# Moving the ConvFFN pool by 64 bytes, one adaLN unit from TensorE to VectorE, and widened products in the second half of a ConvFFN

## The chip, the cores and the metric

The kernel runs on one core of a Trainium2 chip. The metric is the device time of one execution in microseconds (us), lower is better; several executions are summed up by their median. Times inside the program come from one profiled execution and count from the start of its span.

## The reference

The program is one inference step of a two-layer diffusion backbone in float32 with D_MODEL 2048. Two groups of 128 tokens, a context pass and a denoising step, share all weights, so each weight block meets 256 token columns. Layer 0 mixes tokens with latent attention beside grouped-query attention, layer 1 with differential attention; each mixer is followed by a gated ConvFFN. Cut to what matters here:

```python
def conv_ffn(h, w_up, w_conv, b_conv, w_down):
    u = h @ w_up                                  # 2048 -> 2 x 5632
    up = jnp.pad(u, ((0, 0), (1, 1), (0, 0)))
    u = up[:, :-2] * w_conv[0] + up[:, 1:-1] * w_conv[1] + up[:, 2:] * w_conv[2] + b_conv
    gate, val = u[..., :D_FF], u[..., D_FF:]
    return (jax.nn.silu(gate) * val) @ w_down     # 5632 -> 2048

for l in range(DEPTH):                            # DEPTH = 2
    mod = jax.nn.silu(cond) @ w_ada[l] + b_ada[l] # 2048 -> 6 x 2048: the adaLN vectors
    sh1, sc1, gt1, sh2, sc2, gt2 = jnp.split(mod[:, None, :], 6, axis=-1)
    h = rmsnorm(x, g_norm_mix[l]) * (1 + sc1) + sh1
    x = x + gt1 * mixer(h)
    h = rmsnorm(x, g_norm_ffn[l]) * (1 + sc2) + sh2
    x = x + gt2 * conv_ffn(h, w_ffn_up[l], w_ffn_conv[l], b_ffn_conv[l], w_ffn_down[l])
```

## The kernel before

**Products.** Activations lie with features on partitions and 256 columns (128 of each group). To keep float32 accuracy with TensorE's fast format, each activation and each weight is split in a high part and a low part. A product of 2048 input features is 16 blocks of 128x128 weights with three matmuls each: `wh` with the high activations, `wh` with the low ones, `wl` with the high ones, so 48 matmuls of 256 columns, written by `gemm`. In every matmul the 128x128 weight block is loaded first, and 256 activation columns are streamed past it; the weight load of the next matmul runs beside the streaming of this one.

**Splitting the weights.** A weight tile `raw` of 1 MB arrives by a DMA from SP's queue. ScalarE casts it to `wh` (line 249) and VectorE subtracts to get `wl` (line 250), in halves of 1024 columns. In layer 0's ConvFFN a second way takes part of that off VectorE: of every five tiles, two have their second half split by transfer. `prepare` (lines 292 to 303) has ScalarE cast `farh` and write `-farh` into `farl`, and POOL issues a DMA that adds the raw weights from memory onto `farl`. These `farh`/`farl` buffers live in the ConvFFN's own pool.

**The ConvFFN** (`ffn`) goes through its 5632 hidden features in two halves (`q` = 0, 1). In each half `up` makes 22 gate and 22 value products (44 x 48 = 2112 matmuls of `hx` with up-weights), convolves them and splits the result into 22 tiles `g`; `down` makes 16 products of those 22 tiles with the down-weights (16 x 22 x 3 = 1056 matmuls). A list `wider` lets the first matmul of a few products stream 32, 16, 8, 4 and 2 columns more than 256. The added columns are not read. Before the change the list is used up in the first five of these products of each layer's first half. The mixer of layer 1 has a similar list, `push`, after each attention step.

**Addresses.** Each pool is laid out in the order in which its tags are first asked for; a pad of `SHIFT` = 320 bytes comes first in several pools. Within a partition the built program puts `hx` at byte 27264, the four `wh` from 104128 and the four `wl` from 120512 (steps of 4096), and in the ConvFFN pools of both layers `cv` from 148096 and the `g` tiles from 151168 (steps of 2048); in layer 0's also `farh` at 212608 and 216704 and `farl` at 220800 and 224896. Modulo 512 this is 128 for `hx`, `g`, `farh` and `farl`, and 192 for `wh` and `wl`. All steps from block to block and from high to low part are multiples of 512.

**The adaLN vectors** are made in units of 512 outputs of one (layer, vector j, quarter q), beside the other work, in two ways. A unit in `ROWS` is computed on TensorE: 16 matmuls of 512 columns (`sum_rows`), then a copy, four transposes and a reduction. A unit in `FEATS` is computed on VectorE alone, in eight steps of one fused multiply-and-sum over 128x2048 (line 499), for which four 1 MB tiles `araw` are loaded by SP. `pump` hands out these steps after each product at a fixed rate (`FRATE` for VectorE's, `RATE` for TensorE's), up to the limits in `FLIMIT` and `RLIMIT`. At three places (`modulated`) TensorE waits for a normalisation, and one `ROWS` unit is computed there between products.

**Order.** The framework's scheduler sets the order of each engine's instructions from its own simulation, except where `keep_order` pins it. A late `farl` therefore stops TensorE at the matmul that needs it.

Of the kernel before, what the change touches and what calls it, by code (L numbers as in the profile page):

```python
# [18 lines left out]
P = 128  # L19
# [32 lines left out]
NEARLY = _AT["bada"][0] + 2 * KD  # L52
WARM = 9
RATE = {"in0": 0.35, "in": 0.5, "in3": 0.25, "heads": 0.72, "out0": 0.62, "c": 0.36, "outc": 0.36}
FRATE = [{"up": 0.9, "down": 1.8}, {"up": 0.7, "down": 1.42}]
LEAD = (9, 3)
PEW = {"heads": 1.0, "out0": 1.0, "c": 1.0}
QUIET = [4, 3, 3]
LATE = 3
# [2 lines left out]
WIDER = (32, 16, 8, 4, 2)  # L62
# [15 lines left out]
ROWS = [(0, j, q) for q in range(4) for j in (1, 0)]  # L78
ROWS += [(0, j, q) for j in (2, 4) for q in range(4)]
ROWS += [(0, 5, 0)]  # L80
ROWS += [(1, 4, 0), (1, 3, 0)]
FEATS = [(0, 5, 1), (0, 5, 2), (0, 5, 3)]
FEATS += [(1, j, q) for j in (1, 0) for q in range(4)]
FEATS += [(1, 2, q) for q in range(4)]
FEATS += [(1, 5, q) for q in range(4)]
DEEP = [[(0, 3, q) for q in range(4)], [(1, 4, q) for q in range(1, 4)] + [(1, 3, q) for q in range(1, 4)]]
RLIMIT = {"ab": 16, "ffn0": 17, "c": 19, "ffn1": 19}
FLIMIT = {"ab": 0, "ffn0": 15, "c": 15, "ffn1": 19}

SIDE = {"in3": 0.4, "heads": 1.6, "out0": 1.8, "c": 2.2, "outc": 2.0}  # L90
UW = NT + 2
# [4 lines left out]
def step_kernel(ctx: ExitStack, tc: tile.TileContext, A: dict):  # L96
# [45 lines left out]
    def T_(pl, shape, tag, dt=F32, bufs=None):  # L142
        kw = {} if bufs is None else {"bufs": bufs}
        return pl.tile(shape, dt, tag=tag, name=nm(tag), **kw)
# [490 lines left out]
    def pump(rows, feats=0.0, until=None, beside=True):  # L635

        until = until or RLIMIT[stage[0]]
        step()
# [304 lines left out]
    def mixer_ab(hx, beside):  # L943
        l = 0
        with tc.tile_pool(name="ab", bufs=1) as ab:
# [297 lines left out]
            with tc.tile_pool(name="abh", bufs=1) as hp:  # L1243
                ada["pew"] = PEW["heads"]

# [91 lines left out]
    def out_ab(o, st, u, beside, rp):  # L1337
        l = 0
        rows = raw_rows(u, l, 1)
        ensure(l, 2)  # L1340
        ada["pew"] = PEW["out0"]
        W = Weights(A["w_out_ab"], KD, 1)
# [184 lines left out]
    def ffn(hx, W, ready, turn, l, st):  # L1527
        xh, xl = (lambda k: hx[:, k, :NT]), (lambda k: hx[:, k, NT:2 * NT])
        wider = list(WIDER)
        long = len(ready) > 3  # L1530

        def product():
            if ready:
                return ready.pop(0)
            if in_order:
                return gemm(W.chunk(), xh, xl, between=in_order.pop(0))
            if wider:
                n = NT + wider.pop(0)
                return gemm(W.chunk(), xh, xl, more=lambda k: hx[:, k, :n])
            return gemm(W.chunk(), xh, xl)  # L1540

        WD = Weights(A["w_down"][l], KQ, TB)
        cw = ada["cw"]
        with tc.tile_pool(name=f"ffn{l}", bufs=1) as fp, banks(f"pffn{l}") as pf:
            feat["home"], feat["pool"] = fp, pf
            feat["due"] = 0.0
            in_order = [{}, {}] + turn + [{}]
            T_(fp, [P, SHIFT // 4], "pad")

            def conv(m):  # L1550
                early = bool(ready)
                pin = keep_order if early else lambda i: i
                if len(ready) > 4 - 2 * long:
                    W.ahead(pin)
                ps = product()
                y = T_(fp, [P, NT], "cv", bufs=3)
                pin(act.activation(y, ps, AF.Identity, scale=cw[:, 1, m:m + 1], bias=cw[:, 3, m:m + 1]))  # L1557
                y3 = y.rearrange("p (g t) -> p g t", g=2)
                p3 = ps.rearrange("p (g t) -> p g t", g=2)
                pin(dve.scalar_tensor_tensor(out=y3[:, :, 1:], in0=p3[:, :, :T - 1],  # L1560
                                             scalar=cw[:, 0, m:m + 1], in1=y3[:, :, 1:],
                                             op0=ALU.mult, op1=ALU.add))
                pin(dve.scalar_tensor_tensor(out=y3[:, :, :T - 1], in0=p3[:, :, 1:],  # L1563
                                             scalar=cw[:, 2, m:m + 1], in1=y3[:, :, :T - 1],
                                             op0=ALU.mult, op1=ALU.add))
                if early and ready and not long:
                    W.ahead(pin)
                return y

            def up(q):  # L1570
                gs = []
                for i in range(q * KQ, (q + 1) * KQ):
                    rate = 0 if i < LATE else FRATE[l]["up"]
                    fine[0] = False
                    gate = conv(i)
                    pump(0, rate)
                    val = conv(NFF + i)
                    pump(0, rate)
                    act.activation(gate, gate, AF.Silu)
                    dve.tensor_tensor(out=val, in0=gate, in1=val, op=ALU.mult)  # L1580
                    g = T_(fp, [P, ROW], "g", F32R, bufs=KQ)
                    split(g[:, :NT], g[:, NT:2 * NT], val)
                    gs.append(g)
                    if i == LATE - 1:
                        load_row()
                return gs

            def down(gs, q):
                u, rows = None, None
                if q == NQ - 1 and l < NL - 1:  # L1590
                    u = raw_tile(keep, "hx")
                    rows = raw_rows(u, l + 1, 0)
                for c in range(KD):
                    quiet = q == NQ - 1 and c >= KD - QUIET[0]
                    fine[0] = quiet
                    if q == 0:
                        ensure(l, 5, [c // 4])
                    ps = gemm(WD.chunk(), lambda k: gs[k][:, :NT], lambda k: gs[k][:, NT:2 * NT])
                    if l == NL - 1 and q == NQ - 1 and c == KD - 1:
                        last_residual(ps, l, 1, c, st)  # L1600
                    else:
                        residual(ps, l, 1, c, st if q == NQ - 1 else None)
                    if rows:
                        rows(c)
                    if l == NL - 1 and q == NQ - 1 and c in EARLY:
                        act.activation(x[:, c], x[:, c], AF.Identity, scale=C("gfin")[:, c:c + 1])
                    pump(0, 0 if quiet else FRATE[l]["down"])
                return u

            for q in range(NQ):  # L1610
                if l == 0:
                    at, n = 2 * KQ * q, KQ * KD // TB
                    W.go_far(fp, at + LEAD[q], at + 2 * KQ, at + 2 * KQ)
                    WD.go_far(fp, n * q + 3, n * q + n, n * q + n - 6 * q)
                gs = up(q)
                u = down(gs, q)
            while feat["i"] < FLIMIT[stage[0]]:
                feature_step()
            return u
# [26 lines left out]
    with tc.tile_pool(name="cc", bufs=1) as cp, banks("pc") as ppool["ada"]:  # L1646
# [6 lines left out]
        st = stat_init()  # L1653
        ada["pew"] = PEW["c"]
        u = mixer_c(cp, hx, W, begun[0], st)
# [155 lines left out]
```

## Time and profile before

| | us |
|---|---|
| median of 3 executions | 2321.04 (2319.64 to 2321.44) |
| the profiled execution: time | 2326.57 |
| its span | 2324.8 |
| TensorE busy in the span | 2292.3 (99%) |
| VectorE, ScalarE, POOL busy | 1888.9, 1231.6, 227.8 |

In the profile an instruction's busy time overlaps the next one's on TensorE, since matmuls are pipelined; the pace of a stretch is read from the start times of successive matmuls, or from the length of a stretch and the number of matmuls that the code puts in it. Layer 0's ConvFFN runs from about 473 to 1193 us (its second half begins at 819), the mixer of layer 1 from about 1197 to 1595, and layer 1's ConvFFN from about 1615 to 2312 (first `down` from 1833.7, second `up` from 1953.4, second `down` from 2192.7). PE is the matmul stream, PEld the weight loads, SP and POOL issue DMAs.

### The profile page before, as it was taken

Reading aid. Unit: us, or ns where it says so; the run is one execution under the profiler, and the core shown is the slowest. Engines: PE = TensorE matmul, PEld = TensorE weight load, DVE = VectorE, ACT = ScalarE, POOL = GpSimd, SP = SyncE. Lnnn points to the kernel's source line nnn. Section 1 sums busy time; section 2 is a strip of 40 time slices with the busy share of each in tenths; the row PEclk is TensorE's granted clock in tenths of the full one; section 3 lists DMA queues with packets and bytes.
Section 4 is the critical chain, followed back from the end, with each engine's and each line's share of the span. In section 5 each row is a group of like instructions: output and inputs, shape, how many; then the busy total and the mean of one; then the engine's idle time right before and its main releaser. Section 6 shows DMA issues by size and latency. Waiting matters only on the chain.

```text
span 2324.8 us, 47335 instructions
## 1 busy us (share of the span) xinstructions
PE 2292.3 (99%) x19388; PEld 2209.0 (95%) x19388; DVE 1888.9 (81%) x2975; ACT 1231.6 (53%) x1999; POOL 227.8 (10%) x281
## 2 busy tenths in 40 slices
PE   8899999999999999999999999999999999999998
PEld 6788878999999999999999999999999999999998
DVE  4668979889888998989978989998999965666654
ACT  4346555675554455555565455557655434555543
POOL 0012111300000000000230000024000000000011
PEclk9999999999999999999999999999999999999999
DMA  9988879789889999998977887766767655555553
GB/s 380 366 335 307 327 287 366 290 296 305 293 301 318 350 318 305 304 311 291 325 262 268 338 277 272 257 217 214 253 259 269 257 200 198 188 195 200 188 194 127
DMA packets 106313, 639.68 MB, mean 275 GB/s; under 512 B 11440, under 2 KB 19568, under 8 KB 39536
## 3 DMA queue, kind: packets, MB, share of 16 engines
q1 hardware_dynamic: 99904, 614.11, 71.1%
q0 software_dynamic: 6192, 22.55, 5.3%
q8 instruction: 152, 2.49, 0.4%
q14 instruction: 65, 0.53, 0.1%
HBM read 631.86 MB, written 4.75 MB: 274 GB/s over the span
## 4 chain that ended last, share of the span: by engine, by line
PE 94%; DVE 2%; DMA 2%; POOL 1%; ACT 1%; issue 0%; SPq 0%; DVEq 0%; ACTq 0%; POOLq 0%
PE acc L111 89%; PE ada L111 3%; PE att L111 2%; DMA kvb<-w_ada 1%; DVE wl L250 1%; PE att L114 1%; DMA farl<-w_up 0%; PE misc L111 0%; DMA araw<-w_ada 0%; POOL dev L833 0%; DVE hx L551 0%; PE ada L114 0%; DVE x L1668 0%; POOL hxc L837 0%; ACT wh L249 0%
## 5 line engine op out<-in xcount | busy, mean ns | idle before, releaser
L111 PE MATMUL acc<-hx,wh 128*128 128x256 f32 (+1 forms) x6784 | 1188.8, 280 | 5.2 <-ACT wh L249 1.7
L249 ACT CAST wh<-raw 128x1024 fp32r<-128x1024 f32 (+2 forms) x791 | 749.7, 961 | 765.7 <-PE acc L111 637.4
L250 DVE TENSOR_TENSOR wl<-raw,wh 128x1024 fp32r<-128x1024 f32 (+2 forms) x791 | 876.3, 1121 | 264.6 <-ACT wh L249 260.8
L111 PEld LDWEIGHTS acc<-hx,wh 128*128 128x128 f32 x6784 | 1032.8, 189 | 24.0 <-issue 8.5
L111 PE MATMUL acc<-hx,wl 128*128 128x256 f32 (+1 forms) x3392 | 946.0, 279 | 4.7 <-DVE wl L250 4.4
L111 PEld LDWEIGHTS acc<-hx,wl 128*128 128x128 f32 x3392 | 639.5, 189 | 8.1 <-DVE wl L250 6.3
L111 PE MATMUL acc<-g,wh 128*128 128x256 f32 x2608 | 452.7, 279 | 0.0
L111 PEld LDWEIGHTS acc<-g,wh 128*128 128x128 f32 x2608 | 396.6, 189 | 0.0
L111 PE MATMUL acc<-g,wl 128*128 128x256 f32 x1304 | 362.5, 278 | 0.0
L499 DVE CUSTOM_DVE_ANT_0 junk<-araw,condb 128x2048 f32<-128x2048 f32 x152 | 349.5, 2299 | 1.3 <-DMA araw<-w_ada 1.3
L111 PEld LDWEIGHTS acc<-g,wl 128*128 128x128 f32 x1304 | 245.1, 188 | 0.0
L111 PE MATMUL acc<-hxc,wh 128*128 128x256 f32 (+1 forms) x1056 | 188.9, 281 | 0.0
L111 PEld LDWEIGHTS acc<-hxc,wh 128*128 128x128 f32 x1056 | 161.7, 188 | 1.0 <-issue 0.8
L212 POOL TENSOR_TENSOR sqacc<-sqacc,sq 128x256 f32<-128x256 f32 x62 | 73.1, 1178 | 878.6 <-ACT sq L208 878.4
L111 PE MATMUL acc<-hxc,wl 128*128 128x256 f32 (+1 forms) x528 | 146.8, 278 | 0.0
L1557 ACT ACTIVATE cv<-acc,convw 128x256 f32<-128x256 f32 x169 | 94.3, 558 | 19.9 <-PE acc L111 19.7
L111 PEld LDWEIGHTS acc<-hxc,wl 128*128 128x128 f32 x528 | 99.5, 189 | 0.2
L111 PE MATMUL acc<-wh,hxc 128*128 128x256 f32 (+1 forms) x512 | 94.3, 282 | 0.8 <-DVE nt L844 0.8
L111 PE MATMUL acc<-hx,farh 128*128 128x256 f32 x480 | 88.6, 285 | 0.0
L551 DVE CUSTOM_DVE_ANT_0 hx<-block,condb 128x1024 fp32r<-128x1024 f32 x65 | 79.4, 1222 | 6.8 <-DMA block<-w_ada 6.3
L1563 DVE SCALAR_TENSOR_TENSOR cv<-acc,convw,cv 128x254 f32<-128x254 f32 x169 | 81.1, 480 | 3.5
L1560 DVE SCALAR_TENSOR_TENSOR cv<-acc,convw,cv 128x254 f32<-128x254 f32 x169 | 80.5, 477 | 3.3 <-ACT cv L1557 3.3
(275 smaller groups left out, 2280.3 us busy)
## 6 DMA issues: line engine op xcount, KB each, us to landing
raw<-w_up SPq DMA_DIRECT2D x176, 1024.0 KB, 5.3
araw<-w_ada SPq DMA_DIRECT2D x136, 1024.0 KB, 6.9
raw<-w_down SPq DMA_DIRECT2D x88, 1024.0 KB, 5.0
raw<-w_in_c SPq DMA_DIRECT2D x48, 1024.0 KB, 6.6
block<-w_ada SPq DMA_DIRECT2D x41, 512.0 KB, 5.9
raw<-w_in_ab SPq DMA_DIRECT2D x18, 1024.0 KB, 9.2
raw<-w_out_ab SPq DMA_DIRECT2D x16, 1024.0 KB, 8.1
raw<-w_out_c SPq DMA_DIRECT2D x16, 1024.0 KB, 6.1
```

The source lines that it names most:

```text
L111: return self.placed(nc.tensor.matmul(*a, **kw))
L114: return self.placed(nc.tensor.transpose(*a, **kw))
L212: eng.tensor_tensor(out=st["acc"], in0=st["acc"], in1=sq, op=ALU.add)
L249: pin(act.copy(out_hi, src))
L250: pin(dve.tensor_tensor(out=out_lo, in0=src, in1=out_hi.bitcast(F32), op=ALU.subtract))
L499: keep_order(dve.tensor_tensor_reduce(out=T_(feat["pool"], [P, D], "junk"), in1=feat["row"][:, c], in0=feat["raw"].rearrange("p g n -> p ( ...
L551: keep_order(dve.tensor_tensor_reduce(out=self.junk, in0=self.raw, in1=self.row[:, c].rearrange("p (g n) -> p g n", g=2), scale=1.0, scala ...
L1557: pin(act.activation(y, ps, AF.Identity, scale=cw[:, 1, m:m + 1], bias=cw[:, 3, m:m + 1]))
L1560: pin(dve.scalar_tensor_tensor(out=y3[:, :, 1:], in0=p3[:, :, :T - 1], scalar=cw[:, 0, m:m + 1], in1=y3[:, :, 1:], op0=ALU.mult, op1=ALU.add))
L1563: pin(dve.scalar_tensor_tensor(out=y3[:, :, :T - 1], in0=p3[:, :, 1:], scalar=cw[:, 2, m:m + 1], in1=y3[:, :, :T - 1], op0=ALU.mult, op1=A ...
```

## The change

Three things change.

1. A pad of `FARAWAY` = 16 floats (64 bytes), tag `farpad`, is asked for right behind the first pad in the ConvFFN pool, in both layers. In the built program this moves every buffer of that pool by 64 bytes: `cv`, all `g` tiles and the broadcast condition in both layers, and `farh` (212672, 216768) and `farl` (220864, 224960) in layer 0. Modulo 512, `g`, `farh` and `farl` are now at 192; `hx` stays at 128, `wh` and `wl` at 192.
2. Unit (1,4,0) goes from `ROWS` to `FEATS`: eight more steps on VectorE in layer 0's ConvFFN, with rates 0.95 and 1.9 in place of 0.9 and 1.8 to fit them in. Unit (1,3,0) takes its place inside `modulated` ahead of layer 1's mixer, and no unit is left to TensorE within that mixer.
3. In layer 0, the second half's first five `up` products are widened too.

```diff
-FRATE = [{"up": 0.9, "down": 1.8}, {"up": 0.7, "down": 1.42}]
+FRATE = [{"up": 0.95, "down": 1.9}, {"up": 0.7, "down": 1.42}]
 LEAD = (9, 3)
+FARAWAY = 16
...
-ROWS += [(1, 4, 0), (1, 3, 0)]
+ROWS += [(1, 3, 0)]
...
-FEATS += [(1, 2, q) for q in range(4)]
+FEATS += [(1, 2, q) for q in range(4)] + [(1, 4, 0)]
...
-RLIMIT = {"ab": 16, "ffn0": 17, "c": 19, "ffn1": 19}
-FLIMIT = {"ab": 0, "ffn0": 15, "c": 15, "ffn1": 19}
+RLIMIT = {"ab": 16, "ffn0": 17, "c": 18, "ffn1": 18}
+FLIMIT = {"ab": 0, "ffn0": 16, "c": 16, "ffn1": 20}
...
             T_(fp, [P, SHIFT // 4], "pad")
 
+            T_(fp, [P, FARAWAY], "farpad")
...
+                if l == 0 and q:
+                    wider.extend(WIDER)
                 gs = up(q)
```

On TensorE the order changes at the border between layer 0's first `down` (products of `g`) and its second `up` (products of `hx`). A row is a source line, an operation, the tile written, the moving and the weight tile, and the shape. Before, the last `down` product ends and the `up` product begins:

```order
L111 MATMUL acc_9711<-g_8228,farh_9536 128x256 x2
L111 MATMUL acc_9711<-g_8228,farl_9537 128x256
L111 MATMUL acc_9711<-g_8357,farh_9536 128x256 x2
L111 MATMUL acc_9711<-g_8357,farl_9537 128x256
L111 MATMUL acc_9796<-hx_5342,wh_9788 128x256 x2
L111 MATMUL acc_9796<-hx_5342,wl_9789 128x256
```

At the same place of the changed kernel, eight blocks earlier:

```order
L112 MATMUL acc_9721<-g_7267,wl_9718 128x256
L112 MATMUL acc_9721<-g_7405,farh_9545 128x256 x2
L112 MATMUL acc_9810<-hx_5342,wh_9802 128x288
L112 MATMUL acc_9810<-hx_5342,wh_9802 128x256
L112 MATMUL acc_9810<-hx_5342,wl_9803 128x256
L112 MATMUL acc_9721<-g_7405,farl_9546 128x256
L112 MATMUL acc_9721<-g_7544,farh_9545 128x256 x2
```

The first three matmuls of the `up` product, the one with 288 columns among them, now stand inside the last `down` product, and 22 matmuls with `far` weights follow them. The next widened matmul (272 columns) opens the second `up` product.

On TensorE in layer 1's mixer, within a product between two attention steps, before (`ada` is the sum of a unit, `araw` its weights):

```order
L111 MATMUL acc_15414<-hxc_14510,wl_15407 128x256
L111 MATMUL acc_15414<-hxc_14510,wh_15410 128x256
L111 MATMUL ada_15441<-araw_14970,condw_79 32x512 x4
L111 MATMUL ada_15441<-araw_15040,condw_79 32x512 x4
L111 MATMUL acc_15414<-hxc_14510,wh_15410 128x256
L111 MATMUL acc_15414<-hxc_14510,wl_15411 128x256
```

And in the changed kernel:

```order
L112 MATMUL acc_15436<-hxc_14537,wl_15429 128x256
L112 MATMUL acc_15436<-hxc_14537,wh_15432 128x256 x2
L112 MATMUL acc_15436<-hxc_14537,wl_15433 128x256
L112 MATMUL acc_15436<-hxc_14537,wh_15432 128x256 x2
L112 MATMUL acc_15436<-hxc_14537,wl_15433 128x256
```

The unit's matmuls are gone here and at a second place further on, and with them its four transposes.

On VectorE at the end of layer 0's ConvFFN the last steps of the moved unit stand where there were none (`junk` is the step's scratch output, `hx` the next layer's operand being written, `x` the residual), in the changed kernel:

```order
L251 TENSOR_TENSOR wl_14087<-raw_13980,wh_14086 128x512 x2
L500 ISA junk_13796,mod_77<-araw_13794,condb_5751 128x2048
L500 ISA mod_77 128x1
L870 SCALAR_TENSOR_TENSOR x_76<-acc_13994,mod_77,x_76 128x128 x2
L251 TENSOR_TENSOR wl_14093<-raw_13980,wh_14092 128x512 x2
L251 TENSOR_TENSOR wl_14175<-raw_14070,wh_14174 128x512 x2
L500 ISA junk_13890,mod_77<-araw_13794,condb_5751 128x2048
```

Before, at the same product:

```order
L250 TENSOR_TENSOR wl_14060<-raw_13953,wh_14059 128x512 x2
L869 SCALAR_TENSOR_TENSOR x_76<-acc_13967,mod_77,x_76 128x128 x2
L250 TENSOR_TENSOR wl_14066<-raw_13953,wh_14065 128x512 x2
L728 SCALAR_TENSOR_TENSOR hx_12805<-x_76,scl_78,hx_12805 128x128 x2
L250 TENSOR_TENSOR wl_14148<-raw_14043,wh_14147 128x512 x2
```

The last two steps of the unit now stand behind the place where all such steps had ended before.

## The prediction

> **What bounds the kernel now.** I read the page first, then the chain of waits in order of time, then TensorE's start times where the chain's pace changes, then each ConvFFN phase in the table of stretches. The page:
>
> ```profile
> PE 2292.3 (99%) x19388; PEld 2209.0 (95%) x19388; DVE 1888.9 (81%) x2975; ACT 1231.6 (53%) x1999; POOL 227.8 (10%) x281
> L499 DVE CUSTOM_DVE_ANT_0 junk<-araw,condb 128x2048 f32<-128x2048 f32 x152 | 349.5, 2299 | 1.3 <-DMA araw<-w_ada 1.3
> ```
>
> TensorE is the bound almost everywhere, so what counts is its pace per matmul. The chain (start us, length us, what) shows three long pieces of product matmuls:
>
> ```profile
> 473.16 205.57 PE acc L111 x1749
> 678.73 11.17 DMA farl<-w_up
> 689.95 505.71 PE acc L111 x4265
> ...
> 1597.25 715.33 PE acc L111 x6296
> ```
>
> 505.71 us over 4265 matmuls is 118.6 ns each, in layer 0's ConvFFN; 715.33 over 6296 is 113.6 ns, in layer 1's. The shape is the same, yet 5 ns differ. TensorE's timeline (start us, length, instruction; x2 is two merged) shows where the faster pace is lost:
>
> ```profile
> 505.35 0.39 PE L111 MATMUL acc<-hx,wh 128*128 128x256 f32 x2
> ...
> 505.69 0.40 PE L111 MATMUL acc<-hx,farh 128*128 128x256 f32 x2
> 505.93 0.28 PE L111 MATMUL acc<-hx,farl 128*128 128x256 f32 x1
> 506.05 0.40 PE L111 MATMUL acc<-hx,farh 128*128 128x256 f32 x2
> 506.29 0.28 PE L111 MATMUL acc<-hx,farl 128*128 128x256 f32 x1
> ...
> 508.56 0.40 PE L111 MATMUL acc<-hx,wh 128*128 128x256 f32 x2
> ...
> 508.92 0.40 PE L111 MATMUL acc<-hx,wh 128*128 128x256 f32 x2
> ```
>
> Up to 505.69 three matmuls take 0.34 us (113 ns each). With the first `far` weights they take 0.36 (120 ns: 505.93 to 506.29), and when `wh` and `wl` return, the pace does not: it stays near 118. So there are two paces for the same operands, and a `far` block throws TensorE out of the faster one. A widened matmul brings it back, in layer 1's ConvFFN with 288 columns and in its mixer with 272:
>
> ```profile
> 1350.58 0.40 PE L111 MATMUL acc<-hxc,wh 128*128 128x256 f32 x2
> ...
> 1350.94 0.41 PE L111 MATMUL acc<-hxc,wh 128*128 128x272 f32 x2
> ...
> 1351.64 0.39 PE L111 MATMUL acc<-hxc,wh 128*128 128x256 f32 x2
> ...
> 1351.98 0.39 PE L111 MATMUL acc<-hxc,wh 128*128 128x256 f32 x2
> ...
> 1631.93 0.40 PE L111 MATMUL acc<-hx,wh 128*128 128x256 f32 x2
> ...
> 1632.28 0.41 PE L111 MATMUL acc<-hx,wh 128*128 128x288 f32 x2
> ...
> 1633.00 0.39 PE L111 MATMUL acc<-hx,wh 128*128 128x256 f32 x2
> ...
> 1633.34 0.28 PE L111 MATMUL acc<-hx,wh 128*128 128x256 f32 x1
> ```
>
> 0.35 to 0.36 us per three before, 0.34 after. The phases, from the table of stretches (from:to, length, PE busy and count, PEld, DVE, ACT, POOL, clock, DMA share, GB/s):
>
> ```profile
> 505.70:687.50 181.80, 181.80 (x1540) 181.77 (x1538) 159.17 (x206) 102.26 (x139) 10.37 (x12) 1.00 0.90 302
> 693.70:819.00 125.30, 125.30 (x1058) 125.30 (x1058) 112.66 (x133) 54.28 (x54) 6.90 (x8) 1.00 0.95 332
> 819.00:1068.60 249.60, 249.60 (x2115) 249.60 (x2114) 225.32 (x289) 139.03 (x189) 13.86 (x16) 1.00 0.90 306
> 1068.60:1193.20 124.60, 124.60 (x1058) 124.60 (x1057) 112.97 (x162) 67.02 (x113) 21.28 (x19) 1.00 0.84 293
> 1633.70:1833.70 200.00, 200.00 (x1767) 200.00 (x1766) 184.65 (x240) 109.23 (x149) 0.00 (x0) 1.00 0.70 256
> 1833.70:1953.40 119.70, 119.70 (x1059) 119.70 (x1058) 77.94 (x94) 47.38 (x47) 0.00 (x0) 1.00 0.60 213
> 1953.40:2192.70 239.30, 239.30 (x2114) 239.30 (x2113) 162.15 (x218) 126.83 (x174) 0.00 (x0) 1.00 0.56 194
> 2192.70:2312.40 119.70, 119.70 (x1058) 119.70 (x1057) 61.08 (x85) 52.49 (x73) 16.20 (x14) 1.00 0.47 163
> ```
>
> They are, in order: layer 0's first `up` from its first `far` block, its first `down`, second `up`, second `down`; then layer 1's first `up` from the widening on and its other three. Layer 1 keeps 113.3 ns (239.3/2112) through all four, with VectorE 92% busy in the first of these rows. Layer 0's second `up` has 118.2 (249.6/2112); with its 16 `far` halves (two tiles of five, from the fourth on) of 24 matmuls at 120, the other 1728 take 117.8.
>
> **What sets the pace.** Modulo 512 bytes, the streamed `hx` and `g` are at 128 and `wh`, `wl` at 192, 64 apart, while `far` is at 128, 0 apart. The address of the weights alone is not it: in the transposed products of layer 1's mixer the weights are `hxc` (128 modulo 512), the streamed tile is `wh`, 64 apart again, and the faster pace holds:
>
> ```profile
> 1338.05 0.39 PE L111 MATMUL acc<-wh,hxc 128*128 128x256 f32 x2
> ...
> 1338.39 0.39 PE L111 MATMUL acc<-wh,hxc 128*128 128x256 f32 x2
> ```
>
> I take it that 0 apart costs 120 ns and that 64 apart has both paces.
>
> **The change part by part.** The pad moves `far`, which mends layer 0's `up`: `hx` at 128 against `wh` and `far` at 192. But it moves `g` as well, in both layers: `g` at 192 against `wh`, `wl` and `far` at 192 is 0 apart in every matmul of every `down`.
>
> - Layer 0, first `up`: 1540 matmuls at 113.3 instead of 181.8 us: 174.5, so -7.3.
> - Layer 0, first `down`: 1056 at 120 is 126.7 against 125.3: +1.4. Second: 126.7 against 124.6: +2.1.
> - Layer 0, second `up`: the 288-column matmul stands within the last `down` product with 22 `far` matmuls behind it, so I count the first product at 118. The 272-column one that opens the second product flips the pace, as at 1350.94. 2112 at 113.3 plus 48 x 5 ns plus about 0.1 for the added columns is 239.7 against 249.6: -9.9.
> - Layer 1, first `down`: 126.7 against 119.7: +7.0. It leaves the slower pace, and nothing widens the second `up` of layer 1. So that one takes 2112 x 117.8 = 248.8 against 239.3: +9.5. Second `down`: +7.0.
> - The unit taken off TensorE, from the chain within the mixer:
>
> ```profile
> 1269.39 5.72 PE acc L111 x49
> 1275.12 1.85 PE ada L111 x16
> ...
> 1307.20 1.85 PE ada L111 x16
> ...
> 1310.57 11.16 PE acc L111 x97
> ...
> 1347.56 16.60 PE acc L111 x145
> ...
> 1384.20 5.84 PE acc L111 x50
> ```
>
> From 1269.39 to 1310.57 are 41.18 us and to 1347.56 another 36.99, where a head without the unit takes 36.64 (1347.56 to 1384.20): 4.5 + 0.4 = -4.9.
>
> - The unit put on VectorE: 8 x 2.30 = 18.4 us. In layer 0's second `up`, 44 x 0.05 = 2.2 of these steps add 5.1 us to 225.3 while the phase shrinks to 239.7: 96% busy, from 90%. The 92% of layer 1's first `up` cost TensorE nothing, so I price it at 0, with little cover left. Its 4 MB of loads on SP's queue and the faster pace lift the DMA share from 0.90 to about 0.95, what the first `down` has now.
>
> What is late next are the `farl` transfers. One was late already (timeline, and the tile's line):
>
> ```profile
> DMA to landing us min/median/max: 5.3/8.4/12.1
> 689.95 0.38 PE L111 MATMUL acc<-hx,farl 128*128 128x256 f32 x1 [2.19 <-DMA farl<-w_up]
> ```
>
> With products 4% shorter and queues fuller, such a wait gets longer or comes again: between 0 and 2 us in the likely case; I take 0.6, nearer to nothing, since the profile has a single such wait.
>
> Sum: -7.3 + 1.4 - 9.9 + 2.1 + 7.0 + 9.5 + 7.0 - 4.9 + 0.6 = +5.5. The profiled execution took 2326.57, so it would take 2332.1; against the median of 2321.04 that is 2326.5. About 0.2% (4.6 us) is what a measurement of this kernel tells from no change.
>
> [...]
>
> **The rivals.**
>
> 1. *Harmless `g`* (faster). If both tiles at 192 do not disturb each other as both at 128 do, layer 0 runs at 113.3 throughout: -7.3 - 9.9 - 5.6 - 4.9 (each `down` at 119.7), less 4.9 for the unit: -32.6, so 2288. For it: no row shows both at 192. Against it: the distance is the same 0.
> 2. *Late transfers undo the gain* (slower). A wait at an early `far` block of an `up` throws TensorE into the slower pace until the next widening. If it comes at the first of the second `up`, some 9 of the 9.9 us go and 2.2 for the wait itself: 2338. It decides when a landing there takes longer than about 9 us: the one in the chain took 11.17, and TensorE waited 2.19 of them. The median is 8.4.
> 3. *Addresses don't matter*, `far` is slow for being written by transfers. Then the unit's -4.9 is left and a faster pace for the second `up` until its first `far` block, about 1 us: 2315. Against it: `farh`, which ScalarE writes as it writes `wh`, is as slow.
> 4. *Distance 0 costs only the slower pace*, 118, in a `down`. Each `down` then takes 1056 x 117.8 = 124.4: layer 0 gives -17.2 - 0.9 - 0.2, layer 1 +4.7 + 9.5 + 4.7, the unit -4.9: -4.3, so 2317, the lower edge of no change. Against it: 120 in the `far` run shown.
>
> **How the numbers follow.** Forecast 0.55 (within it the edge of 0.2% lies 0.8 us below the centre: 0.35 slower, 0.20 same); rival 1 0.15 (faster), rival 2 0.15 (slower), rival 3 0.07 (faster 0.06, same 0.01), rival 4 0.08 (same 0.05, faster 0.03). Together faster 0.24, same 0.26, slower 0.50. The range, 2314 to 2340, takes in all but rival 1. The likeliest case alone spans 2320 to 2333: a pace read wrong by 1 ns over the 4224 matmuls of `down` is 4.2 us, and the wait for `farl` may go (2.2) or come again (2.2).
>
> **What would show it.** Right: in layer 0's `up` phases 113 ns also in `far` blocks, 120 in all four `down` phases, 118 in layer 1's second `up`, mixer heads all near 36.6 us. Wrong: layer 1 still at 113.3 throughout (rival 1), `far` blocks of `up` still at 120 (rival 3), waits for `farl` early in an `up` (rival 2), or waits for `wl`, if VectorE at 96% runs dry.

## The result, and the profile after

The changed kernel took 2336.91 us (median of 5 executions, 2330.22 to 2338.53) against 2321.44 us for the kernel before in the same rounds (5 executions, 2319.64 to 2324.32). The ratio is 1.0062, with a 95% interval from 1.0045 to 1.0078: slower, by more than the 0.2% that a measurement can tell. The forecast was 2326.5, range 2314 to 2340; the side and the range were right, the centre was 10.4 us too low.

The profiled execution is the fastest of the five: 2330.22 us, span 2328.5, 3.7 us over the profiled one of before. What follows reads that execution. First the page: TensorE's busy time fell by 4.0 us though the span grew by 3.7.

```profile
PE 2288.3 (98%) x19352; PEld 2205.5 (95%) x19352; DVE 1904.0 (82%) x2990; ACT 1227.2 (53%) x1998; POOL 233.9 (10%) x281
```

The table of stretches of the changed kernel (from:to, length, then busy time and count of PE, PEld, DVE, ACT, POOL, then clock, DMA share, GB/s). The rows are layer 0's first `up` from its first `far` block, first `down`, second `up`, second `down`; then layer 1's first `down` and second `up`:

```profile
504.20:686.70 182.50, 179.05 (x1563) 178.37 (x1562) 166.12 (x216) 101.57 (x140) 10.37 (x12) 1.00 0.93 311
686.70:814.50 127.80, 127.56 (x1061) 127.16 (x1060) 117.92 (x138) 55.76 (x57) 6.89 (x8) 1.00 0.97 337
814.50:1063.90 249.40, 245.20 (x2111) 244.02 (x2110) 226.72 (x292) 137.86 (x188) 13.86 (x16) 1.00 0.92 310
1063.90:1190.60 126.70, 126.70 (x1058) 126.70 (x1058) 122.13 (x172) 66.97 (x115) 26.47 (x19) 1.00 0.88 304
...
1823.30:1950.00 126.70, 126.70 (x1059) 126.70 (x1057) 78.25 (x94) 47.08 (x47) 0.00 (x0) 1.00 0.56 203
1950.00:2189.40 239.40, 239.40 (x2115) 239.40 (x2114) 162.09 (x218) 126.82 (x174) 0.00 (x0) 1.00 0.55 193
```

Phase by phase, the difference between the two profiled executions adds up to the 3.7 us:

| stretch | before | after | difference |
|---|---|---|---|
| up to layer 0's ConvFFN (ends at) | 472.9 | 471.4 | -1.5 |
| first `up`, all of it | 220.8 | 215.3 | -5.5 |
| first `down` | 125.3 | 127.8 | +2.5 |
| second `up` | 249.6 | 249.4 | -0.2 |
| second `down` | 124.6 | 126.7 | +2.1 |
| between the ConvFFNs | 422.1 | 414.3 | -7.8 |
| layer 1: first `up` | 218.4 | 218.4 | 0.0 |
| first `down` | 119.7 | 126.7 | +7.0 |
| second `up` | 239.3 | 239.4 | +0.1 |
| second `down` | 119.7 | 126.7 | +7.0 |

Nothing is changed ahead of layer 0's ConvFFN; the other runs reach it between 472.6 and 473.5 us, so the first row is a difference between executions.

The two `down` phases of layer 1 cost 14 us, as forecast: 126.7/1056 is 120.0 ns a matmul, with no wait in them and every other engine less than 62% busy. The `far` blocks of layer 0's `up` do keep the faster pace now. In TensorE's timeline, three matmuls take 0.34 us on both sides of the border at 504.22:

```profile
503.77 0.28 PE L112 MATMUL acc<-hx,wl 128*128 128x256 f32 x1
...
504.11 0.28 PE L112 MATMUL acc<-hx,wl 128*128 128x256 f32 x1
504.22 0.39 PE L112 MATMUL acc<-hx,farh 128*128 128x256 f32 x2
504.45 0.28 PE L112 MATMUL acc<-hx,farl 128*128 128x256 f32 x1
```

What I had wrong is at the other border, in layer 1 from the first `down` to the second `up`, where nothing is widened:

```profile
1949.52 0.28 PE L112 MATMUL acc<-g,wl 128*128 128x256 f32 x1
...
1949.88 0.28 PE L112 MATMUL acc<-g,wl 128*128 128x256 f32 x1
1950.00 0.40 PE L112 MATMUL acc<-hx,wh 128*128 128x256 f32 x2
1950.24 0.28 PE L112 MATMUL acc<-hx,wl 128*128 128x256 f32 x1
...
1950.58 0.28 PE L112 MATMUL acc<-hx,wl 128*128 128x256 f32 x1
```

With the last triple of `g` and the first of `hx` the spacing is 0.36 us (1949.52, 1949.88, 1950.24), from then on 0.34 (1950.58): one triple behind the border TensorE is in the faster pace by itself.

Layer 0's second `up` gained nothing, though it too should run faster. Its idle time is one part. TensorE's waits in layer 0's ConvFFN were one, of 2.2 us, before (the 2.19 at 689.95); now they are nine (what was waited for: us in all, times, longest):

```profile
PE acc L112 <- DMA farl<-w_up: 3.8, 4, 1.5
PE acc L112 <- DVE wl L251: 2.1, 3, 0.9
PE acc L112 <- DVE cv L1566: 1.7, 2, 1.1
```

The other part is its pace, from the table of stretches with pieces of the second `up` that hold no wait:

```profile
840.00:890.00 50.00, 50.00 (x427) 50.00 (x426) 46.85 (x62) 30.19 (x42) 3.46 (x4) 1.00 0.98 342
900.00:950.00 50.00, 50.00 (x444) 50.00 (x443) 44.41 (x60) 27.56 (x38) 2.59 (x3) 1.00 0.95 302
968.00:1018.00 50.00, 50.00 (x427) 50.00 (x426) 42.99 (x56) 26.95 (x38) 3.46 (x4) 1.00 0.91 298
```

427 matmuls in 50 us are the slower pace, 444 the faster one. The phase began at the faster pace (178 matmuls in the 20 us from 817.00). Between the pieces the pace changes where TensorE is held up. At the first `far` block of the phase the third matmul, the first one that needs `farl`, takes 0.39 us instead of 0.28 and sets back what follows by 0.1 us (0.34 us from 838.64 to 838.98, then 0.46 to 839.44), and TensorE goes on at the slower pace. The trace names no wait there, but POOL issued the transfer of that `farl` at 828.37, and it took 10.6 us to land, until just when TensorE came to it. The wait that ends at 896.11, in the fifth block, brings it back to the faster one; the wait that ends at 966.05 leaves it at the slower one again. Timeline, and the line of the `farl` tile for that one transfer:

```profile
838.64 0.28 PE L112 MATMUL acc<-hx,wl 128*128 128x256 f32 x1
...
838.98 0.39 PE L112 MATMUL acc<-hx,farl 128*128 128x256 f32 x1
...
839.44 0.28 PE L112 MATMUL acc<-hx,farl 128*128 128x256 f32 x1
...
896.11 0.39 PE L112 MATMUL acc<-hx,farl 128*128 128x256 f32 x1 [0.33 <-DMA farl<-w_up]
...
966.05 0.39 PE L112 MATMUL acc<-hx,wl 128*128 128x256 f32 x1 [0.79 <-DVE wl L251]
```

```profile
DMA to landing us min/median/max: 10.6/10.6/10.6
```

### The profile page after: what moved, and what is told of

It reads as the page before. It is cut to its first block, busy times and chain, and to the rows that moved or that the text cites. A ratio compares the mean times of both kernels' runs of the same rounds, so it can differ in the third digit from the quotient of the medians.

```text
span 2328.5 us, 47301 instructions
## 1 busy us (share of the span) xinstructions
PE 2288.3 (98%) x19352; PEld 2205.5 (95%) x19352; DVE 1904.0 (82%) x2990; ACT 1227.2 (53%) x1998; POOL 233.9 (10%) x281
## 4 chain that ended last, share of the span: by engine, by line
PE 90%; DMA 4%; DVE 3%; ACT 1%; issue 1%; POOL 1%; SPq 0%; DVEq 0%; ACTq 0%; POOLq 0%
PE acc L112 85%; PE ada L112 2%; PE att L112 2%; DMA farl<-w_up 1%; DVE wl L251 1%; DMA kvb<-w_ada 1%; DVE junk L500 1%; DMA raw<-w_in_ab 1%; PE att L115 1%; DMA farl<-w_down 0%; DMA araw<-w_ada 0%; DMA raw<-w_up 0%; PE misc L112 0%; DVE hx L552 0%; ACT wh L250 0%
## 5 line engine op out<-in xcount | busy, mean ns | idle before, releaser
L112 PE MATMUL acc<-hx,wh 128*128 128x256 f32 (+1 forms) x6784 | 1175.8, 279 | 7.0 <-ACT wh L250 1.7
L112 PEld LDWEIGHTS acc<-hx,wl 128*128 128x128 f32 x3392 | 638.4, 188 | 11.1 <-DVE wl L251 9.3
L112 PE MATMUL acc<-g,wh 128*128 128x256 f32 x2608 | 469.9, 284 | 0.1
L112 PEld LDWEIGHTS acc<-g,wh 128*128 128x128 f32 x2608 | 406.9, 192 | 0.3 <-ACT g L250 0.3
L112 PE MATMUL acc<-g,wl 128*128 128x256 f32 x1304 | 368.9, 284 | 0.0
L500 DVE CUSTOM_DVE_ANT_0 junk<-araw,condb 128x2048 f32<-128x2048 f32 x160 | 367.0, 2294 | 0.0
L112 PEld LDWEIGHTS acc<-g,wl 128*128 128x128 f32 x1304 | 250.4, 192 | 0.0
L213 POOL TENSOR_TENSOR sqacc<-sqacc,sq 128x256 f32<-128x256 f32 x62 | 78.4, 1264 | 882.3 <-ACT sq L209 882.0
L300 ACT CAST farh<-raw 128x1024 fp32r<-128x1024 f32 x43 | 45.2, 1051 | 77.2 <-DMA raw<-w_up 59.8
L1566 DVE SCALAR_TENSOR_TENSOR cv<-acc,convw,cv 128x254 f32<-128x254 f32 x169 | 80.9, 479 | 2.9
```

Source lines behind the costliest of these rows:

```text
L112: return self.placed(nc.tensor.matmul(*a, **kw))
L213: eng.tensor_tensor(out=st["acc"], in0=st["acc"], in1=sq, op=ALU.add)
L300: act.copy(wh, raw[:, 8 * P:n * P])
L500: keep_order(dve.tensor_tensor_reduce(out=T_(feat["pool"], [P, D], "junk"), in1=feat["row"][:, c], in0=feat["raw"].rearrange("p g n -> p ( ...
```

## The experiments

The first four separate the parts of the change. `prepare` is the function that asks for the buffers of the transfers.

**e1: only the transfers' buffers move, `g` stays.** The changed kernel with the pad asked for behind `g` and ahead of `farh`:

```diff
+    padded = []
...
+                    if "far" not in padded:
+                        padded.append("far")
+                        T_(self.far, [P, FARAWAY], "farpad", bufs=1)
...
-            T_(fp, [P, FARAWAY], "farpad")
```

> The changed kernel with the 64-byte pad placed between g and the far buffers, so that far moves and g stays where it was; unit move and widening are kept. Theory A (the distance of streamed tile and weights sets the pace: 0 apart 120 ns, 64 apart 113 or 118): all four down phases leave 120, layer 1's two go from 126.7 back to 119.7 us, together -14.0, layer 0's two from about 127 to 120 at best, -14 more: 2336.9 - 28 = 2309, or up to 2316 if the faster down makes more farl transfers late. Rival B (the changed kernel's loss is the extra unit and its loads, not g): stays within 5 us of 2337.

Measured: 2317.07 us, ratio to before 0.9974 (0.9964 to 0.9985). The rows of layer 0's ConvFFN and of layer 1's first `down`:

```profile
473.50:1191.50 718.00, 700.24 (x6074) 697.50 (x6073) 660.22 (x853) 386.53 (x528) 55.91 (x57) 0.99 0.92 312
...
1827.50:1947.20 119.70, 119.70 (x1058) 119.70 (x1057) 77.96 (x94) 47.39 (x47) 0.00 (x0) 1.00 0.59 213
```

Layer 1's `down` phases are back at 119.7 and 119.6: the 14 us come from where `g` lies (`cv` and the broadcast condition stay with it, but TensorE reads neither in a `down`). The time is 1 us above the range of theory A and far from B. In layer 0 the products became 11.1 us shorter than in the changed kernel (TensorE busy 700.2 against 711.3), but the ConvFFN only 1.2 (718.0 against 719.2): 17.8 us are idle now.

**e2: the pad alone.** The kernel before with the pad where the change has it, without the moved unit and the wider products:

```diff
+FARAWAY = 16
...
+            T_(fp, [P, FARAWAY], "farpad")
```

> The kernel before with the pad of the change alone (g and far both move), no unit moved, no widening mid-way. Both theories: layer 1's down phases +7.0 each, layer 1's second up stays at 113 ns. What differs is layer 0's up. Theory A1 (the faster pace alone makes farl late): several waits of 0.5 to 2 us in the second up as in the changed kernel, which then takes about 249 us: 2321.4 + 14 + 3.5 - 6 = 2333. Theory A2 (the moved unit's steps and loads make farl late): at most two waits, second up about 241 us: 2321.4 + 14 + 3.5 - 7 - 9 = 2323.

Measured: 2332.75 us, ratio 1.0040 (1.0028 to 1.0053). Rows of layer 0's ConvFFN and of the stretch between:

```profile
472.70:1189.50 716.80, 708.89 (x6074) 707.46 (x6073) 644.57 (x835) 385.78 (x528) 59.85 (x57) 1.00 0.90 307
1189.50:1608.70 419.20, 417.83 (x3529) 408.37 (x3529) 376.58 (x673) 242.19 (x488) 74.93 (x92) 1.00 0.75 265
```

The pad alone makes the kernel slower: each `down` of layer 1 takes 126.7 us. The time is that of A1, but not for its reason: layer 0's second `up` took 244.1 us here, without any widened matmul, and not 249 as in the changed kernel.

**e3: the unit alone.** The kernel before with the unit on VectorE, its rates and limits as in the diff of the change, and no pad.

> The kernel before with unit (1,4,0) moved to VectorE, its rates and limits, and nothing else. If the unit's matmuls are all that counts: -4.9, 2316.5, with heads of the mixer all near 36.6 us and layer 0's ConvFFN as long as before (720 us from 473 to 1193). If the extra steps and loads cost TensorE waits there: 2321 or more, with waits for farl or wl in layer 0's ConvFFN.

Measured: 2321.60 us, ratio 0.9993 (0.9983 to 1.0002): no change, as the second expectation has it. The rows of layer 0's ConvFFN and of the stretch between:

```profile
473.30:1195.30 722.00, 717.60 (x6074) 716.55 (x6073) 660.41 (x853) 386.77 (x528) 60.35 (x57) 1.00 0.92 310
1195.30:1609.60 414.30, 412.67 (x3494) 406.55 (x3493) 375.41 (x670) 241.63 (x487) 76.72 (x92) 1.00 0.74 258
```

The stretch between is 7.8 us shorter than before, as in the changed kernel. Only 4.9 of that belong to the unit: e2, without it, has 419.2 there. The other 2.9 are the output projection of layer 1's mixer, 642 matmuls that ran at 118.5 ns before (76.1 us) and at 114.1 in the changed kernel (73.3 us). By the lengths of the stretch they had the faster pace here and in e2 too, and the slower one in e1, where it takes 417.7. The unit's gain on TensorE is real, and layer 0's ConvFFN gives part of it back: 722.0 us against 720.3, with 4.4 us idle (722.0 less 717.6) instead of 2.2.

**e4: only the transfers' buffers move, nothing else.** The kernel before with e1's pad.

> The kernel before with the pad between g and far alone: only far moves. Theory A with no late transfers: layer 0's ConvFFN at 113.3 throughout, -7.3 - 9.9 - 5.6 - 4.9 = -27.7, 2294. Theory A1 (the faster pace alone makes farl late): waits and lost pace give 5 to 15 us of that back, 2299 to 2309. If far is slow for another reason than its distance: 2321.

Measured: 2315.80 us, ratio 0.9970 (0.9957 to 0.9983), the lowest median of the kernels that compute everything, though its interval overlaps that of e1; it beats the kernel before and the changed one. But it is far from the 2294 that its products alone would give, and above the 2299 to 2309 expected with late transfers. Its row of layer 0's ConvFFN, and the two longest entries of TensorE's waits there:

```profile
472.80:1185.70 712.90, 697.25 (x6074) 693.92 (x6073) 643.29 (x835) 386.55 (x528) 55.74 (x57) 1.00 0.91 308
```

```profile
PE acc L112 <- DMA farl<-w_up: 7.8, 5, 2.4
PE acc L112 <- DMA farl<-w_down: 5.0, 5, 2.9
```

For the kernel before, the same row of the table of stretches reads

```profile
472.90:1193.20 720.30, 718.11 (x6074) 717.88 (x6073) 643.85 (x835) 388.80 (x528) 54.35 (x57) 1.00 0.89 305
```

TensorE is busy 20.9 us less and idle 13.5 us more (15.7 against 2.2). So two thirds of the faster products come back as waits, ten of them for `farl`. e1 against e4 also prices the unit on VectorE (the widening beside it does nothing, see e11): layer 0's ConvFFN is 5.1 us longer (718.0 against 712.9), about what the unit saves in the mixer. Of these, 2.1 us are idle time (17.8 against 15.7), as in e3; the other 3.0 are matmuls at the slower pace, and one execution of each can't say whether the unit brings them.

The next four ask why the transfers land late. Two theories: the DMA queues are full there, with a share of 0.9 and more (D), or VectorE is too busy and hands on its buffers too late (V).

**e5: fewer loads.** e4, with the units on VectorE loading one tile in four:

```diff
-        if c == 0:
+        if feat["t"] == 0:
             feat["raw"] = T_(wpool, [P, 4, 512], "araw", bufs=2)
```

> The kernel with far alone moved (2315.8), but VectorE's units load one 1 MB tile in four and use it four times; this leaves out three quarters of the adaLN weights of these units, so only its time is of use. All VectorE steps stay. Theory D (farl and raw are late because the DMA queues are full): the loads that are gone free about a fifth of the traffic, waits for farl fall from 12.8 to under 3 us, layer 0's ConvFFN from 713 to about 692, total near 2295. Theory V (they are late because VectorE frees the raw tiles late): waits and time stay, 2312 to 2318.

Measured: 2305.16 us, ratio 0.9924 (0.9899 to 0.9950). Layer 0's ConvFFN and its second `up` after 890 us (table of stretches), then the line of the `farl` tile:

```profile
472.60:1177.60 705.00, 700.18 (x6073) 699.56 (x6072) 642.79 (x835) 388.48 (x528) 58.06 (x57) 1.00 0.77 245
...
890.00:1053.20 163.20, 163.20 (x1388) 163.20 (x1387) 148.10 (x192) 92.55 (x126) 9.52 (x11) 1.00 0.77 245
```

```profile
DMA to landing us min/median/max: 5.3/5.7/11.0
```

With VectorE as busy as in e4 (642.8 us) and the DMA share at 0.77 instead of 0.91, idle time falls from 15.7 to 4.8 us (705.00 less 700.18), two waits of them for `farl`, and the median landing from 9.4 to 5.7 us. So with fewer loads in the queues `farl` lands sooner and most of the idle time goes, as D has it. The time is some 10 us above the 2295 expected (the ConvFFN 705 instead of 692), and 3.5 us of waits for `farl` are left instead of under 3. The larger rest is pace: from 890 us on the second `up` ran at 117.6 ns (163.2/1388) without a wait, and the second `down` at 117.8 (124.4/1056).

**e6: shorter steps on VectorE.** e4, each step over 256 of its 2048 columns, with the loads as they were.

> The kernel with far alone moved (2315.8), but each of VectorE's unit steps works on 256 of its 2048 columns, which leaves out the rest of those sums. All loads stay. Theory V (VectorE frees the raw tiles late): with about 2 us less in each step, waits for farl fall under 3 us, layer 0's ConvFFN to about 692, total near 2295. Theory D (the DMA queues): waits for farl stay near 12.8 us and the time at 2312 to 2318.

Measured: 2328.45 us, ratio 1.0018 (1.0005 to 1.0031), slower than e4 although VectorE has 204 us less to do in layer 0's ConvFFN. Its row there, and the first two of TensorE's waits:

```profile
473.30:1197.20 723.90, 705.62 (x6074) 701.43 (x6073) 438.76 (x835) 383.62 (x528) 51.20 (x57) 1.00 0.88 304
```

```profile
PE acc L112 <- DVE cv L1568: 7.5, 6, 1.6
PE acc L112 <- DVE wl L251: 3.8, 5, 0.8
```

One of V's expectations is met: no wait for `farl` is left, and its median landing is 7.3 us instead of 9.4, though all loads are made. But TensorE is idle for 18.3 us (723.9 less 705.62), more than in e4, and the time rises: V falls as the cause of the idle time as a whole. How much of `farl`'s lateness is VectorE's stays open, since with shorter steps the order on VectorE and ScalarE changes as well, and the waits are now for other work.

**e7: the transfers start sooner.** e4, with the tiles that feed a transfer loaded in two halves, the transfer's half first:

```diff
-            for i in range(parts):
+            for i in range(parts)[::-1 if back else 1]:
...
-                self.begun.append(self.load())
+                far = self.at in self.span and self.at % 5 in (1, 3)
+                self.begun.append(self.load(2, back=True) if far else self.load())
```

> The kernel with far alone moved (2315.8), and the tiles whose second half goes by transfer are loaded in two DMAs of 512 KB, that half first, so that its cast and transfer start some 2 us earlier. All is computed. If the chain from raw's landing to farl's is what is late (waits of 0.5 to 2.9 us in 10 of 43 transfers): most waits go, 2303 to 2308. If the transfers are held up by full queues whenever they start: no change, 2313 to 2318.

Measured: 2321.73 us, ratio 0.9987 (0.9974 to 1.0001), above e4 and above both expectations. The waits for `farl` fell to 4.3 us and their median landing to 8.1, but TensorE waited 5.9 us for `wl` and 3.9 for `cv` in their stead; layer 0's ConvFFN took 719.2 us. Here the earlier start at nearly equal traffic (a DMA share of 0.91 and 306 GB/s in layer 0's ConvFFN, against 0.91 and 308 in e4) moved the wait to VectorE's work. The run doesn't tell D from V.

**e10: e1 with e7's loads.**

> The same earlier start of the transfers, on the changed kernel with g left where it was (2317.1): unit on VectorE and widening mid-way included. All is computed. If late transfers are what took back the unit's and the pace's gain: a few us below the kernel without the unit, 2299 to 2304. If the unit's steps and loads themselves take it back: not below that one, 2306 or more.

Measured: 2318.14 us, ratio 0.9983 (0.9971 to 0.9995), within the interval of e1 and as the second expectation has it: the earlier start gains nothing. Layer 0's ConvFFN took 717.7 us.

The last three go back to addresses and to the pace.

**e8 and e9: other distances.** The kernel before with the pad in layer 1 alone, of 192 bytes (e8) or 32 bytes (e9), so that `g` there is 128 above or 32 below `wh` and `wl` modulo 512:

```diff
+FARAWAY = 48
...
+            if l == 1:
+                T_(fp, [P, FARAWAY], "farpad")
```

(48 floats in e8, 8 in e9.)

> The kernel before with a pad of 192 bytes ahead of g in layer 1 alone: g there comes to 320 modulo 512, 128 bytes away from wh and wl (at 192), hx stays at 128, 64 away. If only equal addresses modulo 512 (or 256) cost 120 ns, each down of layer 1 takes 119.7 us, as before, or 124.4 at the slower pace, and the time is that of before to +10. If what counts is the distance modulo 128, 128 apart is as good as 0 apart: each down takes 126.7 us, the second up 239.4, and the time is before +14.

> The kernel before with a pad of 32 bytes ahead of g in layer 1 alone: g there comes to 160 modulo 512, 32 away from wh and wl. If the cost is one of equal distance modulo 64 or 128 alone, each down of layer 1 takes 119.7 us as before. If what counts is in which half of 128 bytes an operand lies (0 to 63 or 64 to 127), g at 32 and wh at 64 modulo 128 are still in different halves: 119.7 also. If it grows as the operands come nearer, each down lies between 119.7 and 126.7, near 123.

Measured, with one execution each: 2334.10 (e8) and 2334.59 us (e9), beside a median of 2323.38 for before on the same chip. Layer 1's first `down` in e8:

```profile
1829.90:1955.30 125.40, 125.40 (x1059) 125.40 (x1059) 78.23 (x94) 47.20 (x47) 0.00 (x0) 1.00 0.58 205
```

and in e9:

```profile
1830.70:1955.70 125.00, 125.00 (x1059) 125.00 (x1058) 78.26 (x94) 47.28 (x47) 0.00 (x0) 1.00 0.57 205
```

The second `down` takes as long (125.3 and 124.9), and the second `up` between them 239.3 and 239.4 us. Of the expectations only the last for e9 is met, a `down` between 119.7 and 126.7 us; its reason, nearness, is not, since 128 apart costs more than 32. All three distances other than 64 cost, but not the same, by the mean over a `down`: 120.0 ns at 0, 118.7 at 128, 118.3 at 32, against 113.3 at 64. So a period of 128 bytes is out, since 128 and 0 differ, and it isn't equality alone that costs. Nor do these two means match the slower pace of 64 apart, 117.8, though they lie near it: no `down` holds a wait (125.40 busy of 125.40, 125.00 of 125.00), and the second stands behind an `up` at 113.3. Whether the pace within such a `down` is one throughout was not shown. Two single distances don't give the rule: only `g` was moved, so its own place isn't told from its distance, and whether these distances have a faster pace as well isn't known.

**e11: no wider products mid-way.** The changed kernel without its third part:

```diff
-                if l == 0 and q:
-                    wider.extend(WIDER)
```

> The changed kernel without the wider first products mid-way. My prediction had the second up of layer 0 enter at 118 ns and be brought to 113 by the widened matmul. By what layer 1 showed (a pace of 113.3 right after a down at 120, with nothing widened), the widening does nothing: layer 0's second up starts at 113.3 here too, and the time is that of the changed kernel, 2330 to 2338, within 3 us of it in the same rounds. If the widening is what holds the fast pace after waits, the second up takes up to 9 us longer and the time is 2340 to 2347. If its waits come by chance alone, the phase is 245 to 255 us.

Measured: 2338.44 us, ratio 1.0064 (1.0046 to 1.0083); the changed kernel has 1.0062 against the same kernel before. The widening does nothing that can be measured. TensorE's timeline at the start of layer 0's second `up` shows the faster pace from the second triple on (0.36 us, then 0.34), with no wider matmul:

```profile
820.24 0.28 PE L112 MATMUL acc<-g,farl 128*128 128x256 f32 x1
...
820.60 0.28 PE L112 MATMUL acc<-hx,wl 128*128 128x256 f32 x1
...
820.94 0.28 PE L112 MATMUL acc<-hx,wl 128*128 128x256 f32 x1
```

Its profiled execution took 2341.03 us, 10.8 more than that of the changed kernel, with the same phases in layer 1 (218.4, 126.7, 239.3, 126.8). Layer 0's ConvFFN took 724.9 instead of 719.2, and the stretch between 417.4 instead of 414.3, close to the 2.8 us that the slower pace of the output projection adds (76.1 less 73.3). In two places of layer 0 TensorE ran at half clock for at least 3 us, the second behind a wait of 1.93 us that ended at 1030.38 (a clock of 0.51 from 1031.5 to 1034.5). The first, in the table of stretches (the clock stands third from the end):

```profile
618.20:621.20 3.00, 3.00 (x16) 3.00 (x16) 1.14 (x1) 3.00 (x4) 0.00 (x0) 0.50 0.76 295
```

## Why the prediction was right, and where it was not

The side and the range came out right. That the sum came near is luck: two of its terms, -9.9 and +9.5, were both wrong and cancel, and two costs were set too low.

- *Layer 0, first `up`, -7.3.* Measured -5.5. The `far` blocks run at 113.3 as said; the rest went to new waits (3.5 us, 182.50 against 179.05 busy) and to a stretch at the slower pace. These took more than the 1.8 us that are missing: the term ended at 687.5, and the phase's last `far` block, 6.2 us up to 693.7 in the kernel before with its wait and its half clock, got shorter too.
- *The four `down` phases, +1.4, +2.1, +7.0, +7.0.* Measured +2.5, +2.1, +7.0, +7.0. 120 ns for `g` on `wh`, `wl` and `far` at the same address modulo 512 was right to a tenth, and e1 shows that it is the address of `g`. Rivals 1 and 4 fall. The same matmuls take 113.3 ns in e1 and 120.0 here; what slows them was not shown. The first `down` has 1.1 us more, of which 0.2 is idle time (127.80 against 127.56 busy).
- *Layer 0, second `up`, -9.9.* This failed: -0.2. The step that failed is that the wider products put TensorE into the faster pace and that it stays there. It enters by itself (e11), and it doesn't stay: six waits take 4.2 us (249.40 against 245.20 busy), and some 115 us of the phase passed at 118, about 4.5 us more than at 113.3.
- *Layer 1, second `up`, +9.5.* This failed: +0.1. I took from layer 0, where the slower pace stays after a `far` block, that it stays after any stretch at distance 0. After a `down` it doesn't, here, in e2 and in e11, nor at the other slow distances of e8 and e9. That the streamed tile changes there, and not behind a `far` block of an `up`, is not enough to explain it. In the kernel before, layer 0's second `up` follows a `far` block of the `down`, so that `hx` takes the place of `g`, and the slower pace stays (0.35 to 0.36 us for three):

```profile
818.87 0.28 PE L111 MATMUL acc<-g,farl 128*128 128x256 f32 x1
...
819.22 0.28 PE L111 MATMUL acc<-hx,wl 128*128 128x256 f32 x1
...
819.57 0.28 PE L111 MATMUL acc<-hx,wl 128*128 128x256 f32 x1
...
819.93 0.28 PE L111 MATMUL acc<-hx,wl 128*128 128x256 f32 x1
```

There `g` and `hx` both lie at 128 modulo 512. Where the faster pace came back behind a `down`, the streamed tile moved from 192, 320 or 160 to 128. That this decides was not tried, and the cause stays open.
- *The unit off TensorE, -4.9.* Right: 4.9 at equal pace of the output projection (e2 against e3), 4.4 between before and e1, which both have it slow. The profiled difference of -7.8 holds 2.9 us for that projection's pace, which the prediction had not seen and which comes and goes between kernels.
- *The unit on VectorE, 0.* This failed. Layer 0's ConvFFN is 1.7 us longer with it in e3 and 5.1 in e1 against e4, some 2 us of either in idle time, and neither pair of kernels clearly gains from the unit. I had judged VectorE's load by layer 1's first `up`, 92% busy at no cost, but there the DMA share is 0.70. The unit's loads, which I had named, had to be priced: e5 shows that fewer loads make the transfers land sooner. No run adds the unit's steps without its loads, so the two aren't told apart. The 96% for VectorE in the second `up` was too high as well: it was 91% (226.72 of 249.40), since the extra steps fell mostly into the two `down` phases (117.92 and 122.13 us busy, from 112.66 and 112.97).
- *Late transfers, +0.6.* Too small: TensorE idles 7.9 us in layer 0's ConvFFN instead of 2.2. Of these, 3.8 us are for `farl`, whose median landing rose from 8.4 to 9.8 us.

Rival 2 came true for this phase more than I gave it credit for. Its point of decision was a landing longer than 9 us at the first `far` block of the second `up`: that transfer took 10.6 us, TensorE was thrown into the slower pace there (838.98), and the phase's gain went. But it took a delay of 0.1 us there and not a wait of 2.2, there were six waits in the phase, and one of them (896.11) ended the slower stretch where the rival had only a widening end it. So its price of some 11 us for this phase was about right (9.7, from -9.9 to -0.2), but made up in another way. Rival 3 is refuted by the row at 504.45 and by e4.

Against the prediction's 2326.5 the median is 10.4 us higher, but the profiled execution only 1.9 lower than its 2332.1. The other four executions of the changed kernel took 5.7 to 8.3 us longer than the profiled one, and no trace of them exists. e11, whose profiled execution took 10.8 us longer at the same order of products but for the widening, shows one way: longer waits in layer 0 (11.0 us instead of 7.6), half clock in two places there (0.50 and 0.51), and a stretch between the ConvFFNs that is 3.1 us longer. That the four executions lost their time so is likely and was not shown.

## What to carry to other kernels

Move one buffer at a time: a pad inside a pool shifts everything behind it, and here one pad cured 5 ns in the matmuls of one stage and put 6.7 ns on those of another, while the same pad behind `g` was a gain. A faster product stage is worth its pace only if the loads of that stage can keep up (in e4, at a DMA share of 0.91, 13.5 of the 20.9 us came back as idle time): look at the DMA share and the landing times in that stage before you count the gain, and price added loads, not only added steps. A pace that has two values for the same code, here 113.3 and 117.8 ns, should enter a forecast as two cases at each border and each wait, not as a rule learnt at one of them.

## What the hardware showed that I had not expected

- The pace of the same matmul, 256 columns streamed past one 128x128 weight tile, changed with where the two operands lie. By their distance modulo 512 bytes it was 120.0 ns at 0, 118.3 at 32, 118.7 at 128 (the last two as means over a `down`, in one execution each), and 113.3 at 64, where 118 occurs too and holds for hundreds of matmuls. The period of 512 is taken, not tested; the cause is open.
- In the changed kernel a wait of TensorE changed the pace in both directions, though operands and addresses stayed the same: from 427 matmuls in 50 us to 444 behind the wait that ends at 896.11, and back to 427 behind the one that ends at 966.05. Behind a delay of 0.1 us (838.98) it went from 0.34 us for three matmuls to 427 in 50 us.
- Half clock came behind some waits of about 2 us and not behind others. In the kernel before, the 2.19 us at 689.95 were followed by 3.4 us of it (table of stretches):

```profile
691.40:694.80 3.40, 3.40 (x19) 3.40 (x18) 3.40 (x5) 0.98 (x2) 0.00 (x0) 0.50 0.95 354
```

In e4 a longer one, 2.40 us, was not, as far as was read: the clock was 1.00 from 687.50 to 689.50 (timeline: 0.46 us to the next `farl` matmul, then 0.35, where three matmuls at half clock took 0.64 in the kernel before, 692.16 to 692.80):

```profile
687.63 0.38 PE L112 MATMUL acc<-hx,farl 128*128 128x256 f32 x1 [2.40 <-DMA farl<-w_up]
...
688.09 0.28 PE L112 MATMUL acc<-hx,farl 128*128 128x256 f32 x1
...
688.44 0.28 PE L112 MATMUL acc<-hx,farl 128*128 128x256 f32 x1
```

What separates the two was not shown.
